# Rotary swap and key duplication by partition copies, one product for a norm's sum, and head norms' squares as float32r pairs

## The chip, the cores and the metric

The kernel runs on one core of a Trainium2 chip. The metric is the time of one execution on the device, in microseconds; the median of several runs counts. Five engines work side by side, each through its own queue in order: TensorE (matrix products; PE in the profile, its weight loads PEld), VectorE (DVE), ScalarE (ACT), GpSimd (POOL) and SyncE (SP), which issues most of the DMAs.

## The reference

Two layers of a diffusion backbone over 256 latent tokens and 256 context tokens, 1024 features. A layer is a half-step SwiGLU, three parallel token mixers with a common input projection, and another half-step SwiGLU. Before each sub-layer stands an RMS norm with a shift and a scale that depend on the condition. In short:

```python
def rmsnorm(x, g):
    return x * lax.rsqrt(jnp.mean(x * x, axis=-1, keepdims=True) + EPS) * g

def adaln(h, m, j, gain):
    return rmsnorm(h, gain) * (1 + m[3 * j + 1]) + m[3 * j]

def apply_rope(x, cos, sin):
    x1, x2 = jnp.split(x, 2, axis=-1)
    return jnp.concatenate([x1 * cos - x2 * sin, x1 * sin + x2 * cos], axis=-1)

# attention: 8 query heads of 64 and 2 key heads, each key head for 4 query heads;
# queries and keys go through rmsnorm over their 64 features, then apply_rope (latent tokens only)
# gated linear attention and mLSTM: 4 heads of 128 each, their outputs go through rmsnorm over 128 features
x = x + 0.5 * m[2] * swiglu(adaln(x, m, 0, g[0]), w13, w2)
x = x + m[5] * mixers(adaln(x, m, 1, g[1]))
x = x + 0.5 * m[8] * swiglu(adaln(x, m, 2, g[2]), w13, w2)
```

In the last layer the context tokens are only needed up to the keys, values and states; its queries, outputs and second half step are computed for the latent tokens alone.

## The kernel before

Features lie on the partitions and the 512 tokens on the columns (`L` = 256 is where the latent tokens begin), so a tile is 128 features by 512 tokens. In the last layer the mixers' outputs and the second half step work on columns 256 to 511 only (`c0 = L`).

Dense products are done as three float32r products (`mm3`, high and low parts of weights and inputs). A weight unit of 128x1024 is loaded by SP, split by ScalarE (`hi`, line 231) and VectorE (`lo`, line 232), and used by 24 products; three units are buffered. Smaller products, and those that form sums over partitions, are plain float32 products through `mm` (lines 149 and 150).

The stages of a layer: the first half step (`ffn`), the mixers (`mixer`), the second half step. In `mixer` the order of the program is: gate columns, gated linear attention (`gla`, two calls that norm two heads each by `head_norm`), the mLSTM (`mlstm`, two calls with two heads each, the same), the first branch of the output projections, values, keys and queries (each tile: a dense product, then `qk_norm`), `attention`, the gates of the attention's branch, the second and third branches, and the output projection. `attention` first makes `kd`, a copy of each key head on both halves of the partitions (product with the table `dup`), and turns `kd` and the four query tiles with `rope`: a product with the permutation table `perm` swaps the halves of 32 features within each head, and VectorE multiplies by the tables of cosine and sine and adds. Scores, softmax and transposes follow for each key head and block of 128 queries.

`square` forms the squares of the residual's eight tiles as they are finished; those of tiles 0 to 5 are added up by GpSimd, and `norm_sums` sums that total and the last two tiles over the features with three products with `ones_d`. `neg2rstd` then takes -2/sqrt of it (Ln, Exp and a Newton step), and `exp_ln_tables` loads ScalarE's table set for it behind the last square. At the end of a phase (`turn`) the last output tiles are computed for the context's columns and then for the latent's, with the next norm behind each, so that one stream's norm lies beside the other's products.

The program text gives data flow and priorities. The framework's scheduler fixes the order of every engine's queue when the program is built, prefers what stands earlier in the text, and fills with later work; it also places the tiles in their pools (the pool `tp` of `W()` has 17 buffers) and sets the semaphores.

Of the kernel before, what the change touches and what calls it, by code (L numbers as in the profile page):

```python
# [9 lines left out]
F32 = mybir.dt.float32  # L10
# [22 lines left out]
# columns of w_in, in the order the kernel consumes them (gate block first)  # L33
# [15 lines left out]
# columns of the small per-layer parameters  # L49
# [8 lines left out]
# shape-only float tables  # L58
CT = {}
# [18 lines left out]
def hybrid_backbone_kernel(ctx: ExitStack, tc: tile.TileContext, xT, cc, small, tables, lmask, crow, modw, modt,  # L78
# [42 lines left out]
    def tt(o, a, b, op):  # L121
        V.tensor_tensor(o, a, b, op)  # L122

    def act(o, i, f, **k):
        return A.activation(o, i, f, **k)  # L125
# [9 lines left out]
    def load(o, i):  # L135
        """a load; those of the start in the order of the program, and some later ones behind them."""
        d = nc.sync.dma_start(o, i)
        if loads and late[0] < 24:
            order(d, loads[-1])
        if starting[0]:  # L140
            loads.append(d)
        else:
            late[0] += 1

    def exp_ln_tables(after):
        """load the table set that serves both Exp and Ln, behind the activation `after`."""
        order(A.preload_act_table_set("natural_log_exp_and_others"), after, "table set of the next functions")  # L147

    def mm(o, l, r, start=True, stop=True):
        PE.matmul(o, l, r, start=start, stop=stop)  # L150

# [1 line left out]
    ct = res.tile([128, N_CT], F32, name="ct")  # L153
# [5 lines left out]
    ones_h = res.tile([128, 128], F32, name="ones_h")  # L159
# [4 lines left out]
    def C(n, i=None, w=128):  # L164
        o, ww = CT[n]
        return ct[:, o:o + ww] if i is None else ct[:, o + i * w:o + (i + 1) * w]
# [19 lines left out]
    V.memset(ones_h[:], 1.0 / 128)  # L186
    V.memset(ones_1[:], 1.0)
    V.memset(onec[:], 0.0)
# [8 lines left out]
    def load_tables():  # L197
        load(ct[:, 130:], tables[:, 130:])
        for i, n in ((0, 4), (4, 3)):
            t = W()  # L200
            load(t[:, :n * 128], lmask[:, i * 128:(i + n) * 128])
            V.tensor_copy(lm[:, i:i + n, :], t[:, :n * 128].rearrange("p (a b) -> p a b", a=n))
        V.tensor_copy(sel[:], C("selm"))

# [1 line left out]
    behind = []  # L206

    class Unit:
        """a run of weight columns as a float32r pair; each part is one tile or a list of tiles of 512."""
# [31 lines left out]
    def wunit_f(src, n, raw=None):  # L241
        """the same in tiles of the feature pool, for units that are wanted ahead of their turn."""
        raw = wraw(src, n) if raw is None else raw
        his, los = [], []
        with tc.high_priority():
            for a in range(0, n, 512):
                m = min(512, n - a)
                hi, lo = F(F32R), F(F32R)
                A.copy(hi[:, :m], raw[:, a:a + m])
                tt(lo[:, :m], raw[:, a:a + m], hi[:, :m].bitcast(F32), ALU.subtract)  # L250
                his.append(hi)
                los.append(lo)
        return Unit(his, los)

    def ahead(srcs):
        """the first two units of the next phase."""
        return [cols8(wunit(srcs[0], 1024)), cols8(wunit_f(srcs[1], 1024))]
# [11 lines left out]
    def dense_with(w, xs, cs):  # L269
        """one tile of 128 output features over the columns cs; K = 128 * len(xs)."""  # L270
        ps = acc()
        for k, x in enumerate(xs):
            mm3(ps[:, cs], w[k][0], w[k][1], x, cs, k == 0, k == len(xs) - 1)
        return ps
# [4 lines left out]
    def dense_halves(ws, xs, done):  # L279
        """some tiles, one stream after the other: starts before the second stream is there."""  # L280
# [9 lines left out]
    def dense_tokens(src, xs):  # L290
        """512 output features with the tokens on partitions: one tile per chunk."""
# [33 lines left out]
    def start(src):  # L325
        """the first norm, the modulation it needs and the first products, as the weights come in."""
# [29 lines left out]
        def features(k):  # L356
            """modulation of the features 128 * k .., then these features of the norm."""
            with tc.high_priority() if k == 0 else ExitStack():
# [9 lines left out]
                for j in range(2):  # L368
                    mm(pt[:, 2 * j:2 * j + 2], sb[:, 128 * j:128 * j + 128], C("sel2"))
# [25 lines left out]
    def load_cond():  # L395
        """silu of the two conditioning vectors, on every partition."""
# [7 lines left out]
    def mod_vec(l, j, cond):  # L404
        """generator: modulation vector j of layer l on the vector engine, 128 features a step."""
# [46 lines left out]
    def mod_scale(l, j):  # L452
        """-0.5 * gain * (1 + scale) of norm j."""
# [7 lines left out]
    def mod_gate(l, j):  # L461
        """half of the gate of sub-layer j."""
# [10 lines left out]
    def neg2rstd(ms, cs, eps_col, eps):  # L473
        """-2 / sqrt(ms + eps): table value with one Newton step."""
# [11 lines left out]
    def square(k, c):  # L486
        """squares of one tile of the stream c, summed over the tiles but the last two."""
# [4 lines left out]
        elif k < KD - 2:  # L492
            G.tensor_tensor(sums[c.start][0][:, c], sums[c.start][0][:, c], q[:, c], ALU.add)
        else:
            sums[c.start].append(q)
# [6 lines left out]
    def adaln(l, j, c0=0):  # L502
        """norm j of layer l: one call of the result for each stream, behind its last residual."""
# [13 lines left out]
    def norm_sums(c, tabled):  # L517
# [4 lines left out]
        for n, q in enumerate(parts):  # L522
            mm(ms[:, c], ones_d[:], q[:, c], n == 0, n == len(parts) - 1)
# [30 lines left out]
    def turn(late, h, gate, nxt):  # L554
        """the last output tiles of a phase by streams, with the norm of the next phase behind each."""
# [11 lines left out]
    def ffn(l, j, c0, fill, pre, xn, side, nxt, head=None):  # L567
        """one half step; pre: the first weights, nxt: where those of the next phase are."""
# [44 lines left out]
    def log_sigmoid(z, bias, out_t, tmp):  # L613
        """log sigmoid(z + bias) = min(z + bias, 0) - ln(1 + exp(-|z + bias|))."""
# [5 lines left out]

    def head_norm(out, o, cs, gcol, eps_col, eps, tabled=True):
        """-2 * rmsnorm over the partitions of o (PSUM), times gcol."""
        sq = W()
        i = act(sq[:, cs], o[:, cs], AF.Square)
        if tabled:
            exp_ln_tables(i)
        ms = mx()
        mm(ms[:, cs], ones_h[:], sq[:, cs])
# [6 lines left out]
    def gla(l, ft, c0, gq, gk, gv, gb, gw2, gcol):  # L635
# [6 lines left out]
        for d in range(2):  # L642
            z = mx()
            mm(z[:], gw2[:, (2 * d + ft) * 128:(2 * d + ft + 1) * 128], gb[:])
# [13 lines left out]
        # states between chunks  # L658
# [3 lines left out]
        for d in range(2):  # L662
# [17 lines left out]
            for i, c in enumerate(ch):  # L680
                ps = mx()
                for hh in range(2):
                    mm(ps[64 * hh:64 * hh + 64, 0:128], kd[:, i * 128 + 64 * hh:i * 128 + 64 * hh + 64],
                       gv[c][:, hd(2 * ft + hh)])
# [7 lines left out]
        # within chunks  # L692
        att = []
        for hh in range(2):
            ps = mx()
            r = slice(64 * hh, 64 * hh + 64)
            for c in range(q0, 4):
                cc_ = slice(c * 128, (c + 1) * 128)
                mm(ps[:, cc_], gk[r, cc_], gq[r, cc_])
# [3 lines left out]
        for li, s in enumerate(LEVELS):  # L703
# [16 lines left out]
            for hh in range(2):  # L720
                ps = mx()
                r = slice(64 * hh, 64 * hh + 64)
                for c in range(q0, 4):
                    cc_ = slice(c * 128, (c + 1) * 128)
                    mm(ps[:, cc_], ek[r, cc_], eq[r, cc_])
# [4 lines left out]
        # outputs  # L730
# [28 lines left out]
    def conv_silu(l, ps, i, c0):  # L759
        """twice silu(conv(x) + b) of one tile of channels."""  # L760
# [18 lines left out]
    def mlstm_rows(l, gb):  # L779
        selgb = C("selgb")  # L780
        pi, pf = mx(), mx()
        mm(pi[:], selgb[:, 0:128], gb[:])
        mm(pf[:], selgb[:, 128:256], gb[:])
# [22 lines left out]
        # columns r = (head parity within direction q, head pair): index 2 * q + hp  # L806
# [9 lines left out]
        # values at the ends of chunks, spread over the partitions  # L816
# [8 lines left out]
        mm(ps[:, 0:64], ones_1[:], dd[:].rearrange("p a b -> p (a b)"))  # L825
# [14 lines left out]
    def mlstm(l, hp, c0, mq, mk, mv, R, gcol):  # L840
# [6 lines left out]
        for hl, h in enumerate(heads):  # L847
            # states between chunks
# [5 lines left out]
            for d in range(2):  # L854
# [7 lines left out]
                for i, c in enumerate(order[d]):  # L862
                    ps = mx()
                    mm(ps[:, 0:129], kt[:, c * 128:(c + 1) * 128], vs[:, i * 129:(i + 1) * 129])
# [7 lines left out]
            # weights within chunks  # L872
            sc = mx()
            for c in range(q0, 4):
                cc_ = slice(c * 128, (c + 1) * 128)
                mm(sc[:, cc_], mk[h][:, cc_], mq[h][:, cc_])
# [10 lines left out]
        # denominators, one row of 32 per (direction, head)  # L887
        den1, qn = mx(), mx()
        for hl in range(2):
            for d in range(2):  # L890
                q = 2 * d + hl
                rr = slice(32 * q, 32 * q + 32)
                mm(den1[rr, cs], onec[:] if hp == 0 else onec2[:], sw[d, hl][:, cs])
                for c in range(q0, 4):
                    cc_ = slice(c * 128, (c + 1) * 128)
                    if c in before[d]:
                        i = before[d][c]
                        # the sum of keys, column 128 of the state, goes to row hp of 32
                        mm(qn[rr, cc_], Cs[d, hl][:, i * 160 + 128 - hp:i * 160 + 160 - hp], mq[heads[hl]][:, cc_])
                    else:  # L900
                        mm(qn[rr, cc_], zero32[:], mq[heads[hl]][:, cc_])
# [36 lines left out]
    def qk_norm(ps, cs, gcol):  # L938
        x, sq = F(), W()
        V.tensor_copy(x[:, cs], ps[:, cs])  # L940
        exp_ln_tables(act(sq[:, cs], x[:, cs], AF.Square))
        ms = mx()
        mm(ms[:, cs], C("blk"), sq[:, cs])
# [4 lines left out]
    def rope(x):  # L948
        ls = slice(L, T)
        ps = mx()  # L950
        mm(ps[:, ls], C("perm"), x[:, ls])
        t = W()
        tt(t[:, ls], ps[:, ls], C("sin"), ALU.mult)
# [3 lines left out]
    def attention(l, c0, aq, kh, vt):  # L957
        ls = slice(L, T)
        kd = []
        for kv in range(2):  # L960
            ps = mx()
            mm(ps[:], C("dup", kv), kh[:])
            t = W()
            A.copy(t[:], ps[:])
# [7 lines left out]
        for kv in range(2):  # L972
            for qt in range(c0 // 128, 4):
# [7 lines left out]
                for j in range(4):  # L981
# [3 lines left out]
                    mm(ps[:, 0:nk], aq[h // 2][r, qc], kd[kv][r, 0:nk])  # L985
# [171 lines left out]
    def beside(l, j, vecs):  # L1157
        """modulation vectors of later sub-layers, computed beside a half step."""
# [25 lines left out]
def _pack(a, mt, kt):  # L1184
    """(K, M) -> [M tile, partition, k * 128 + m]."""
# [3 lines left out]
def _cols(v):  # L1189
    """a vector of n * 128 features as [partition, n]."""  # L1190
# [3 lines left out]
def _tables():  # L1194
# [23 lines left out]
    # queries on partitions, keys on columns  # L1218
# [4 lines left out]
    # source j on partitions, target i on columns  # L1223
# [113 lines left out]
```

## Time and profile before

| | |
|---|---|
| runs, median of 3 | 2334.57 us (2333.76 to 2335.11) |
| profiled execution, first to last instruction (its span) | 2333.1 us |
| median less the profiled span | 1.5 us |
| TensorE with a record of a product | 2291.4 us, 98% |
| VectorE busy | 1533.6 us, 66% |
| ScalarE busy | 975.1 us, 42% |
| GpSimd busy | 53.2 us, 2% |

The profile is of one execution, whose own time is given as its span only. A matrix product's record is longer than its distance to the next one, because products overlap; so the share of TensorE says where it had nothing to do, and what a product costs is read from the distances of the starts. A float32 product shows as two records of the same form.

### The profile page before, as it was taken

The numbers are of one execution on the slowest core, as the hardware profiler recorded it, in microseconds if no ns is written. First come the engines' busy times: TensorE is split into PE (matmuls) and PEld (weight loads), VectorE is DVE, ScalarE is ACT, GpSimd is POOL, SyncE is SP. The second block draws the span as 40 slices with busy tenths as digits, with TensorE's granted clock in tenths as the row PEclk, the third lists the DMA queues.
The fourth block names the chain that finished last, engine by engine and source line by source line (L and its number), as shares of the span: only waits on it lengthen the run. The fifth ranks groups of instructions, "written<-read, shape, count | busy, mean of one in ns | idle before, by whom it ended". The sixth has DMA issues, their size and how long they took to land. (4 is left out here: it accounts for less than half of the span.)

```text
span 2333.1 us, 32827 instructions
## 1 busy us (share of the span) xinstructions
PE 2291.4 (98%) x12496; PEld 1910.3 (82%) x12496; DVE 1533.6 (66%) x3213; ACT 975.1 (42%) x1569; POOL 53.2 (2%) x65
## 2 busy tenths in 40 slices
PE   7999999999999999999999999999999999999999
PEld 4888888777877667888888898888888788889999
DVE  4686875579865664658833357855545897877755
ACT  4322224445644542342222253222245665745443
POOL 0000001000000000100000000000010000001000
PEclk9999999999999999999999999999999999999999
DMA  7665554212211212436533236655433233335764
GB/s 282 210 200 159 187 187 129 91 48 66 82 55 64 64 46 81 147 111 198 173 113 99 76 115 208 202 160 188 157 114 103 88 100 100 109 120 183 241 199 145
DMA packets 117390, 314.94 MB, mean 135 GB/s; under 512 B 13296, under 2 KB 16240, under 8 KB 117104
## 3 DMA queue, kind: packets, MB, share of 16 engines
q1 hardware_dynamic: 116208, 309.69, 41.3%
q0 software_dynamic: 1024, 3.15, 0.4%
q8 instruction: 98, 1.61, 0.3%
q14 instruction: 60, 0.49, 0.1%
HBM read 308.59 MB, written 4.19 MB: 134 GB/s over the span
## 5 line engine op out<-in xcount | busy, mean ns | idle before, releaser
L231 ACT CAST hi<-raw 128x1024 fp32r<-128x1024 f32 (+2 forms) x446 | 434.6, 977 | 962.7 <-PE acc L150 637.4
L150 PE MATMUL acc<-xh,hi 128*128 128x512 f32 (+1 forms) x2192 | 784.5, 358 | 9.6 <-ACT xh L125 6.3
L150 PE MATMUL acc<-xl,hi 128*128 128x512 f32 (+1 forms) x2192 | 783.9, 358 | 0.2
L150 PE MATMUL acc<-xh,lo 128*128 128x512 f32 (+1 forms) x2192 | 781.7, 357 | 1.6 <-DVE lo L232 1.6
L232 DVE TENSOR_TENSOR lo<-raw,hi 128x1024 fp32r<-128x1024 f32 (+2 forms) x446 | 503.4, 1131 | 322.9 <-ACT hi L231 307.7
L150 PEld LDWEIGHTS acc<-xh,hi 128*128 128x128 f32 x2192 | 415.7, 190 | 76.8 <-ACT xh L125 8.7
L150 PEld LDWEIGHTS acc<-xl,hi 128*128 128x128 f32 x2192 | 415.7, 190 | 66.1 <-issue 8.8
L150 PEld LDWEIGHTS acc<-xh,lo 128*128 128x128 f32 x2192 | 415.7, 190 | 64.4 <-issue 6.7
L150 PE MATMUL acc<-f,hi 128*128 128x512 f32 (+1 forms) x1016 | 352.2, 347 | 0.0
L150 PE MATMUL acc<-f,lo 128*128 128x512 f32 (+1 forms) x896 | 314.1, 351 | 0.0
L415 DVE SCALAR_TENSOR_TENSOR u<-f,f 128x512 f32<-128x512 f32 x448 | 284.6, 685 | 12.7 <-DMA f<-in_modt_dram 12.7
L150 PE MATMUL acc<-t,hi 128*128 128x512 f32 (+1 forms) x824 | 287.1, 349 | 0.0
L150 PEld LDWEIGHTS acc<-f,hi 128*128 128x128 f32 x1016 | 192.2, 189 | 25.0 <-issue 1.2
L150 PEld LDWEIGHTS acc<-f,lo 128*128 128x128 f32 x896 | 169.7, 189 | 22.1 <-issue 0.4
L150 PEld LDWEIGHTS acc<-t,hi 128*128 128x128 f32 x824 | 155.8, 189 | 20.3
L122 DVE TENSOR_TENSOR t<-t,acc 128x512 f32<-128x512 f32 (+1 forms) x90 | 54.9, 610 | 154.8 <-PE acc L150 153.7
L539 DVE SCALAR_TENSOR_TENSOR x<-acc,ggt,x 128x256 f32<-128x256 f32 x136 | 61.1, 479 | 88.5 <-PE acc L150 88.4
L125 ACT ACTIVATE t<-t 128x512 f32<-128x512 f32 (+2 forms) x180 | 93.0, 529 | 58.3 <-DVE t L122 35.7
L122 DVE TENSOR_TENSOR t<-t,f 128x512 fp32r<-128x512 f32 (+3 forms) x172 | 99.2, 585 | 2.9 <-ACT f L313 2.1
L150 PE MATMUL mx<-t,t 64*128 64x128 f32 (+2 forms) x592 | 77.9, 288 | 0.9 <-DVE t L861 0.5
L150 PEld LDWEIGHTS mx<-t,t 64*128 64x128 f32 (+1 forms) x592 | 64.2, 188 | 16.3 <-issue 9.1
L150 PE MATMUL mx<-t,f 128*64 128x256 f32 (+3 forms) x352 | 69.8, 412 | 0.4
(209 smaller groups left out, 2167.3 us busy)
## 6 DMA issues: line engine op xcount, KB each, us to landing
raw<-in_w_dram SPq DMA_DIRECT2D x179, 512.0 KB, 3.6
f<-in_modt_dram SPq DMA_DIRECT2D x256, 256.0 KB, 4.5
raw<-in_win_dram SPq DMA_DIRECT2D x118, 512.0 KB, 3.5
raw<-in_w_dram SPq DMA_DIRECT2D x61, 384.0 KB, 3.1
raw<-in_w_dram SPq DMA_DIRECT2D x61, 320.0 KB, 3.0
raw<-in_wout_dram SPq DMA_DIRECT2D x24, 512.0 KB, 3.5
f<-in_modw_dram SPq DMA_DIRECT2D x32, 256.0 KB, 5.3
raw<-in_wo_dram SPq DMA_DIRECT2D x16, 512.0 KB, 3.8
```

What stands on the lines that cost most here:

```text
L122: V.tensor_tensor(o, a, b, op)
L125: return A.activation(o, i, f, **k)
L150: PE.matmul(o, l, r, start=start, stop=stop)
L231: a = A.copy(hi[:, :n], raw[:, :n])
L232: b = V.tensor_tensor(lo[:, :n], raw[:, :n], hi[:, :n].bitcast(F32), ALU.subtract)
L415: V.scalar_tensor_tensor(junk[:], raw[:], 1.0, cond[s][h][:], ALU.mult, ALU.mult, accum_out=part[:, k, s, h:h + 1])
L539: V.scalar_tensor_tensor(X[m][:, c], ps[:, c], gate[:, m, s:s + 1], X[m][:, c], ALU.mult, ALU.add)
```

## The change

`rope` takes the swap of the halves from four GpSimd copies of 32 partitions by 256 columns each, in place of a product. `attention` makes the duplicated keys with two copies of 64 partitions by 512 columns, one on ScalarE and one on GpSimd, in place of a product and a ScalarE copy from PSUM. `square` adds the last two tiles' squares to the total on VectorE, so that `norm_sums` is left with one product. `head_norm` and `qk_norm` write the square twice, once rounded to float32r, subtract to get the low part, and sum over the partitions with two float32r products (`mean_squares`). The tables `perm` and `dup` are no longer loaded (the load is in two parts), `ones_h` and a copy of the table `blk` become float32r. `tt`, `act` and `mm` become names of the engines' functions themselves, and comments go. The start's norm (`start`) is left as it is.

```diff
+    tt, act, mm = V.tensor_tensor, A.activation, PE.matmul
...
-        load(ct[:, 130:], tables[:, 130:])
+        load(ct[:, 130:skip[0]], tables[:, 130:skip[0]])
+        load(ct[:, skip[0]:], tables[:, skip[1]:])
...
+        V.tensor_copy(blk_r[:], C("blk"))
...
     def square(k, c):
         q = W()
         i = act(q[:, c], X[k][:, c], AF.Square)
         if k == 0:
             sums[c.start] = [q]
         elif k < KD - 2:
             G.tensor_tensor(sums[c.start][0][:, c], sums[c.start][0][:, c], q[:, c], ALU.add)
         else:
-            sums[c.start].append(q)
+            tt(sums[c.start][0][:, c], sums[c.start][0][:, c], q[:, c], ALU.add)
...
         ms = mx()
-        for n, q in enumerate(parts):
-            mm(ms[:, c], ones_d[:], q[:, c], n == 0, n == len(parts) - 1)
+        mm(ms[:, c], ones_d[:], parts[0][:, c], True, True)
         return ms
...
+    def mean_squares(x, w, cs):
+
+        sq, hi, lo = W(), W(F32R), W(F32R)
+        act(hi[:, cs], x[:, cs], AF.Square)
+        i = act(sq[:, cs], x[:, cs], AF.Square)
+        tt(lo[:, cs], sq[:, cs], hi[:, cs].bitcast(F32), ALU.subtract)
+        ms = mx()
+        mm(ms[:, cs], w[:], hi[:, cs], True, False)
+        mm(ms[:, cs], w[:], lo[:, cs], False, True)
+        return ms, i
+
     def head_norm(out, o, cs, gcol, eps_col, eps, tabled=True):
-        """-2 * rmsnorm over the partitions of o (PSUM), times gcol."""
-        sq = W()
-        i = act(sq[:, cs], o[:, cs], AF.Square)
+
+        ms, i = mean_squares(o, ones_h, cs)
         if tabled:
             exp_ln_tables(i)
-        ms = mx()
-        mm(ms[:, cs], ones_h[:], sq[:, cs])
...
     def qk_norm(ps, cs, gcol):
-        x, sq = F(), W()
+        x = F()
         V.tensor_copy(x[:, cs], ps[:, cs])
-        exp_ln_tables(act(sq[:, cs], x[:, cs], AF.Square))
-        ms = mx()
-        mm(ms[:, cs], C("blk"), sq[:, cs])
+        ms, i = mean_squares(x, blk_r, cs)
+        exp_ln_tables(i)
...
     def rope(x):
         ls = slice(L, T)
-        ps = mx()
-        mm(ps[:, ls], C("perm"), x[:, ls])
         t = W()
-        tt(t[:, ls], ps[:, ls], C("sin"), ALU.mult)
+        for i in range(4):
+            j = i ^ 1
+            G.tensor_copy(t[32 * i:32 * i + 32, ls], x[32 * j:32 * j + 32, ls])
+        tt(t[:, ls], t[:, ls], C("sin"), ALU.mult)
...
         for kv in range(2):
-            ps = mx()
-            mm(ps[:], C("dup", kv), kh[:])
             t = W()
-            A.copy(t[:], ps[:])
+            for e in range(2):
+                (A.copy if e == kv else G.tensor_copy)(t[64 * e:64 * e + 64, :], kh[64 * kv:64 * kv + 64, :])
             rope(t)
```

## Rows read from the trace of the kernel before

**Rows 1.** Page: span, and engines' busy time, share and instructions.

```profile
span 2333.1 us, 32827 instructions
...
PE 2291.4 (98%) x12496; PEld 1910.3 (82%) x12496; DVE 1533.6 (66%) x3213; ACT 975.1 (42%) x1569; POOL 53.2 (2%) x65
```

**Rows 2.** Windows: stretch, its length, busy us per engine, granted clock, DMA share, GB/s.

```profile
1800.00:1900.00 100.00, 99.45 (x640) 80.22 (x639) 89.12 (x220) 71.28 (x129) 0.00 (x0) 1.00 0.26 83
...
2000.00:2100.00 100.00, 95.92 (x717) 82.53 (x716) 77.03 (x172) 55.31 (x109) 2.16 (x4) 1.00 0.40 122
```

**Rows 3.** Groups by line and shape, TensorE: count, busy us, mean ns, idle before.

```profile
L150 PE MATMUL mx<-t,ones_d 128*128 128x256 f32 x54 | 15.1, 388 | 0.2 <-ACT t L125 0.2
```

**Rows 4.** Timeline, TensorE: start us, length us, names, shape, records merged.

```profile
390.51 0.28 PE L150 MATMUL acc<-f,f 128*128 128x256 f32 x1
390.63 1.02 PE L150 MATMUL mx<-t,ones_d 128*128 128x256 f32 x4
...
391.61 0.28 PE L150 MATMUL acc<-t,hi 128*128 128x256 f32 x1
...
753.78 0.39 PE L150 MATMUL acc<-xh,hi 128*128 128x512 f32 x1
...
754.46 0.39 PE L150 MATMUL acc<-xh,hi 128*128 128x512 f32 x1
754.71 1.13 PE L150 MATMUL mx<-t,ct 128*128 128x512 f32 x2
755.27 0.79 PE L150 MATMUL acc<-xl,hi 128*128 128x512 f32 x1
755.90 0.40 PE L150 MATMUL acc<-xh,lo 128*128 128x512 f32 x1
...
2002.77 0.28 PE L150 MATMUL acc<-xh,lo 128*128 128x256 f32 x1
2002.91 0.70 PE L150 MATMUL mx<-t,ct 128*128 128x256 f32 x2
2003.26 0.47 PE L150 MATMUL acc<-xh,hi 128*128 128x256 f32 x1
2003.57 0.28 PE L150 MATMUL acc<-xl,hi 128*128 128x256 f32 x1
2003.69 0.28 PE L150 MATMUL acc<-xh,lo 128*128 128x256 f32 x1
```

**Rows 5.** Waits, TensorE: who waited for whom, us in total, times, longest.

```profile
PE mx L1006 <- DVE t L999: 6.7, 7, 1.5
...
PE acc L150 <- ACT xh L125: 6.3, 3, 4.1
```

**Rows 6.** Timeline, a turn's first norm, TensorE and ScalarE.

```profile
1369.83 1.28 ACT L147 ACT_TABLE_LOAD   x1
...
1369.87 0.70 PE L150 MATMUL mx<-t,ones_d 128*128 128x256 f32 x2
...
1371.13 0.48 ACT L125 ACTIVATE t<-mx,kc 128x256 f32<-128x256 f32 x1
```

**Rows 7.** Line 493's durations (min/median/max ns); groups by shape, VectorE.

```profile
L493 POOL TENSOR_TENSOR t<-t,t x45: 725/805/1465, 354.0 to 2126.3; 128x256 f32<-128x256 f32 x45
...
L122 DVE TENSOR_TENSOR t<-t 128x256 f32<-128x256 f32 x56 | 20.5, 418 | 0.0
...
L122 DVE TENSOR_TENSOR t<-t,t 128x512 f32<-128x512 f32 x18 | 12.4, 687 | 14.2 <-ACT t L125 14.0
```

**Rows 8.** Layer 1: timeline (key tile's norm, first scores); chain behind the attention.

```profile
1995.57 0.75 DVE L945 SCALAR_TENSOR_TENSOR f<-f,cols,t 128x512 f32<-128x512 f32 x1
...
2018.15 1.13 PE L150 MATMUL mx<-t,f 64*128 64x512 f32 x4
...
2083.93 45.48 PE acc L150 x375
```

More of the change, by code (lines that the diff above doesn't have):

```diff
@@ L119, in mx @@
         return pmx.tile([128, T], F32, tag="mx", name=nm("mx"))
[L121 to L125, printed above, removed]
+    tt, act, mm = V.tensor_tensor, A.activation, PE.matmul
     no_sync = mybir.DependencyInfo(mybir.DependencyClass.NoSync, mybir.DependencyReason.DATA)
@@ L147, in exp_ln_tables @@
         order(A.preload_act_table_set("natural_log_exp_and_others"), after, "table set of the next functions")
-    def mm(o, l, r, start=True, stop=True):
-        PE.matmul(o, l, r, start=start, stop=stop)
-    ct = res.tile([128, N_CT], F32, name="ct")
+    skip = CT["perm"][0], CT["cos"][0]
+    ct = res.tile([128, N_CT - skip[1] + skip[0]], F32, name="ct")
     sel = res.tile([128, 8], F32R, name="sel")
@@ L158, in hybrid_backbone_kernel @@
     ones_d = res.tile([128, 128], F32, name="ones_d")
-    ones_h = res.tile([128, 128], F32, name="ones_h")
+    ones_h = res.tile([128, 128], F32R, name="ones_h")
+    blk_r = res.tile([128, 128], F32R, name="blk_r")
     ones_1 = res.tile([128, 128], F32, name="ones_1")
@@ L165, in C @@
         o, ww = CT[n]
+        o -= skip[1] - skip[0] if o >= skip[1] else 0
         return ct[:, o:o + ww] if i is None else ct[:, o + i * w:o + (i + 1) * w]
@@ L185, in hybrid_backbone_kernel @@
     V.memset(ones_d[:], 1.0 / D)
-    V.memset(ones_h[:], 1.0 / 128)
     V.memset(ones_1[:], 1.0)
+    V.tensor_scalar(ones_h[:], ones_1[:], 1.0 / 128, None, ALU.mult)
     V.memset(onec[:], 0.0)
@@ L368, in features @@
                 for j in range(2):
-                    mm(pt[:, 2 * j:2 * j + 2], sb[:, 128 * j:128 * j + 128], C("sel2"))
+                    mm(pt[:, 2 * j:2 * j + 2], sb[:, 128 * j:128 * j + 128], C("sel2"), True, True)
                 tt(m[:, :, k, :], pt[:, 0:4].rearrange("p (j s) -> p j s", j=2), bias[:, :, k, :].to_broadcast([128, 2, 2]),
@@ L643, in gla @@
             z = mx()
-            mm(z[:], gw2[:, (2 * d + ft) * 128:(2 * d + ft + 1) * 128], gb[:])
+            mm(z[:], gw2[:, (2 * d + ft) * 128:(2 * d + ft + 1) * 128], gb[:], True, True)
             t1, t2, pr = W(), W(), W()
@@ L683, in gla @@
                     mm(ps[64 * hh:64 * hh + 64, 0:128], kd[:, i * 128 + 64 * hh:i * 128 + 64 * hh + 64],
-                       gv[c][:, hd(2 * ft + hh)])
+                       gv[c][:, hd(2 * ft + hh)], True, True)
                 if i == 0:
@@ L698, in gla @@
                 cc_ = slice(c * 128, (c + 1) * 128)
-                mm(ps[:, cc_], gk[r, cc_], gq[r, cc_])
+                mm(ps[:, cc_], gk[r, cc_], gq[r, cc_], True, True)
             a = W()
@@ L724, in gla @@
                     cc_ = slice(c * 128, (c + 1) * 128)
-                    mm(ps[:, cc_], ek[r, cc_], eq[r, cc_])
+                    mm(ps[:, cc_], ek[r, cc_], eq[r, cc_], True, True)
                 V.copy_predicated(chunk_view(att[hh])[:, q0:4, :],
@@ L781, in mlstm_rows @@
         pi, pf = mx(), mx()
-        mm(pi[:], selgb[:, 0:128], gb[:])
-        mm(pf[:], selgb[:, 128:256], gb[:])
+        mm(pi[:], selgb[:, 0:128], gb[:], True, True)
+        mm(pf[:], selgb[:, 128:256], gb[:], True, True)
         ic, tmp, lf, b, m = W(), W(), W(), W(), F()
@@ L824, in mlstm_rows @@
         ps = mx()
-        mm(ps[:, 0:64], ones_1[:], dd[:].rearrange("p a b -> p (a b)"))
+        mm(ps[:, 0:64], ones_1[:], dd[:].rearrange("p a b -> p (a b)"), True, True)
         eb = sp.tile([128, 8, 8], F32, tag="eb", bufs=1, name=nm("eb"))
@@ L863, in mlstm @@
                     ps = mx()
-                    mm(ps[:, 0:129], kt[:, c * 128:(c + 1) * 128], vs[:, i * 129:(i + 1) * 129])
+                    mm(ps[:, 0:129], kt[:, c * 128:(c + 1) * 128], vs[:, i * 129:(i + 1) * 129], True, True)
                     o = i * 160
@@ L875, in mlstm @@
                 cc_ = slice(c * 128, (c + 1) * 128)
-                mm(sc[:, cc_], mk[h][:, cc_], mq[h][:, cc_])
+                mm(sc[:, cc_], mk[h][:, cc_], mq[h][:, cc_], True, True)
             for d in range(2):
@@ L892, in mlstm @@
                 rr = slice(32 * q, 32 * q + 32)
-                mm(den1[rr, cs], onec[:] if hp == 0 else onec2[:], sw[d, hl][:, cs])
+                mm(den1[rr, cs], onec[:] if hp == 0 else onec2[:], sw[d, hl][:, cs], True, True)
                 for c in range(q0, 4):
@@ L897, in mlstm @@
                         i = before[d][c]
-                        mm(qn[rr, cc_], Cs[d, hl][:, i * 160 + 128 - hp:i * 160 + 160 - hp], mq[heads[hl]][:, cc_])
+                        mm(qn[rr, cc_], Cs[d, hl][:, i * 160 + 128 - hp:i * 160 + 160 - hp], mq[heads[hl]][:, cc_], True, True)
                     else:
-                        mm(qn[rr, cc_], zero32[:], mq[heads[hl]][:, cc_])
+                        mm(qn[rr, cc_], zero32[:], mq[heads[hl]][:, cc_], True, True)
         den, nd = W(), W()
@@ L984, in attention @@
                     ps = mx()
-                    mm(ps[:, 0:nk], aq[h // 2][r, qc], kd[kv][r, 0:nk])
+                    mm(ps[:, 0:nk], aq[h // 2][r, qc], kd[kv][r, 0:nk], True, True)
                     if lat:
```

## Prediction

> **What bounds the kernel now.** I read the page's busy table first [rows 1]: TensorE's records cover 2291.4 of the 2333.1 us span, VectorE's 1533.6, and nothing else comes near. Busy time alone doesn't say that TensorE sets the end, since its records overlap, so I looked at the table by stretches [rows 2] and at start-to-start distances [rows 4]. In the two stretches with the attention and its surroundings TensorE is busy 99.45 and 95.92 of 100 us at a granted clock of 1.00 (the 2.4 GHz level), and dense float32r products follow each other every 0.227 us with 512 columns (753.78 to 754.46 is three) and every 0.12 us with 256. That rhythm is the array at work, not a queue at rest. The view of waits [rows 5] names the rest: 41.7 us (2333.1 - 2291.4) without a record, in small pieces; the probabilities before the attention's transposes cost 6.7 us in 7 waits, the modulated input behind a norm 6.3 in 3. So time that is taken out of TensorE's queue comes off the end, unless a new wait eats it; work added to VectorE, ScalarE or GpSimd is free as long as it lies beside the dense stream.
>
> **What a removed product is worth.** A float32 product shows as two records (27 norm products give the 54 records in [rows 3]). Its price in place [rows 4]: alone in a 512-column stream, the product before it is through at 754.46 + 0.227 = 754.69, and the one behind it begins 0.227 before its successor at 755.90, so at 755.67 (the 755.27 that is listed overlaps): 0.98 us. Alone at 256 columns: 2002.77 + 0.12 = 2002.89 to 2003.57 - 0.12 = 2003.45: 0.56 us. Two in a row at 256 columns: 390.51 + 0.12 = 390.63 to 391.61 - 0.12 = 391.49, so 0.43 each, hence 0.86 for 512 (twice the columns). These are the two ends: 0.43 to 0.56, and 0.86 to 0.98. A float32r pair is taken at the dense price: 2 x 0.12 = 0.24, and 2 x 0.227 = 0.45.
>
> **The change, part by part, on TensorE.**
> 1. Norm sums: nine stream norms (two in each of four turns, one in the last mixer) go from three products to one. The two that go stand mostly as a pair: 9 x 0.86 = 7.7 us.
> 2. Rotary swap: 6 calls in each layer, 12 products of 256 columns gone: 12 x 0.43 to 0.56 = 5.2 to 6.7 us.
> 3. Key duplication: 2 in each layer, 4 of 512 columns: 3.4 to 3.9 us.
> 4. Head norms and query/key norms as pairs: 14 of 512 columns (8 heads and 5 query/key tiles in layer 0, the key tile in layer 1) save 0.86 - 0.45 = 0.41 to 0.53 each, 5.7 to 7.4 us; 12 of 256 columns save 0.43 - 0.24 = 0.19 to 0.32, 2.3 to 3.8 us.
>
> The sum is 24.3 to 29.5 us. These products stand singly and in bunches, so I take the middle, 27.
>
> **What it adds elsewhere.** The pairs add a Square on ScalarE and a subtraction on VectorE to each of 26 norms, and the norm sums 18 adds of 0.42 us on VectorE [rows 7]. A subtraction is 0.69 us with 512 columns and 0.42 with 256 [rows 7], so VectorE gets 14 x 0.69 + 12 x 0.42 + 18 x 0.42 = 22 us. Its fullest stretch has 89.12 us of 100 [rows 2]; there it gets the four gate-attention heads of layer 1, under 2 us. Covered by the dense stream; were it not, 2 us come back.
>
> In the chain of a head norm only the first Square is late: the subtraction and both products lie under the table load of 1.28 us that stands behind the second Square. Rows of the same form: the load runs 1369.83 to 1371.11, the Ln starts at 1371.13, and the norm's product, sent at 1369.87, is through some 0.55 later [rows 6]. What is late next, 0.4 to 0.6 us a norm, is a gating or a rotary step that dense tiles cover.
>
> The norm between phases is the delicate one. For a turn's first stream the last square is now followed by an add (0.42 and about 0.1 of hand-over) ahead of the one product: 1369.87 becomes 1370.4, and the product is through at about 1370.95, still before the Ln at 1371.13. For the second stream the pair (0.86) behind the last square becomes add and product (0.42 + 0.1 + 0.43 = 0.95): 0.1 us late. TensorE waits for a norm in three places now, 6.3 us [rows 5]; nine norms at 0.1 are 0.9 us, and if the whole add were bare, 9 x 0.52 = 4.7 us. I take 1.
>
> The table split costs one DMA issue more on SP, early, in the filler beside the first half step; its bytes fall by 384 columns. Nothing waits there, at most one load is a place later. Three work tiles per norm instead of one press on the 17 buffers of that pool; a late buffer delays ScalarE and VectorE, and TensorE only after the dense tiles between. I count nothing, and leave it to a rival.
>
> **The GpSimd copies.** The trace has no such copy. Nearest rows: GpSimd's add of 128x256 takes 0.725 to 1.465 us, median 0.805 [rows 7], with two inputs where a copy has one; from below nothing excludes a tenth of that. I take 0.6 for 32x256 and 1.2 for the 64x512 half of a key tile (twice the columns), and keep 0.1 to 1.47.
>
> GPSIMD Engine Reference of the Trainium skill, section 1, says that GpSimd's SBUF interfaces are shared with VectorE and suffer from its instructions with two SBUF inputs; the spread from 0.725 to 1.465 agrees. Its section 4.1 puts one-input work at about line rate, which at its 1.2 GHz would be an estimate of 0.21 us for 256 columns plus dispatch: the sum would stay as it is.
>
> Is there room? In layer 1 the normed key tile is ready at 1995.57 + 0.75 = 1996.3, and the first scores start at 2018.15 [rows 8], 21.8 us later. Before the first group of four heads GpSimd must do two large copies and the small ones of four rotary calls (both key tiles, two query tiles): 16 small ones and 2 of double length, 20 units. At 0.6 that is 12 us, at 1.47 29 us. Behind the attention TensorE runs 375 products in 45.48 us [rows 8], 0.121 each; the attention's branch (96) and the output projection (192) need it, the other 87, 10.5 us, don't and could be done earlier. So 32.3 us are free, 1.6 us per unit. The swap now also no longer stands in TensorE's queue, where it waited for the query tiles' dense products. I cost the copies at nothing; without the cover each unit's excess over 1.6 us costs 20-fold in layer 1. Layer 0 has more room: tiles twice as wide.
>
> A late copy also blocks VectorE: the multiply by the sine waits for four copies, 2.4 us (5.9 at 1.47), and the weight splits stand behind it. Three weight units are buffered, 24 x 0.12 = 2.9 us each in layer 1, 8.6 us together: covered.
>
> **Sum.** The profiled execution's span is 2333.1, the runs' median 1.5 above it. 2333.1 - 27 + 1 for the norms + 1 for waits that a new order of the queues brings = 2308.1; with 1.5 outside the span 2309.6, say 2309.5.
>
> **Rivals.**
> A, slower: the GpSimd copies are really slow, because moving data to other partitions is another mechanism than its add. It decides in layer 1, between the normed key tile and the first scores: at c us per unit 20c - 32.3 come back. The gain of 25 is gone at c = 2.9. At c = 4 the time is 2309.5 + 48 = 2357. Against it: the longest add is 1.47 [rows 7], half of what it needs; for it: no row shows a copy to other partitions. 6%.
> GPSIMD Engine Reference of the Trainium skill, sections 1 and 3.2, speaks for A: each of GpSimd's eight cores owns 16 partitions in ordinary work, and data goes from one core to another over links of their own. No run here shows such a copy yet.
> B, half the gain: the queues' order is fixed when the program is built, and the longer chains (two Squares, a subtraction, copies, three buffers) make VectorE or ScalarE late by a microsecond or so where TensorE has no cover, as it is before the attention's transposes now [rows 5]. Twelve rotary calls at 1 us bring 12 back: 2321. For it: VectorE is at 77 to 89% there [rows 2]. 16%.
> C, no effect: within 4.7 us of before. It takes the loss of more than four fifths of 27 us, for instance TensorE just waiting at the same places for longer. The rhythm in [rows 4] speaks against it. 4%.
> D, more: an attention that can start earlier also loses some of the 6.7 us before its transposes, and the upper prices hold: 2333.1 - 29.5 - 5 + 1.5 = 2300. 11%.
> My forecast, 2304 to 2316, has the remaining 63%.
>
> **Range and chances.** 2301 to 2324 holds the forecast, most of B and about half of D, 8 in 10. About 0.2% (4.7 us) is what a measurement of this kernel can tell from no change. Faster: forecast, D and B, 90%; same 4%; slower 6%.
>
> **What would show it.** In the changed profile the norm's 256-column records fall from 54 to 18, those of the swap and the duplication are gone, and TensorE's busy time falls by about 25 us with its idle time near 42. GpSimd's busy time rises by 48 small and 4 large copies; around 0.6 us each proves that part, over 1.6 us refutes it. Waits of TensorE for the rotary's last add, for a subtraction behind a Square, or longer ones for the input behind a norm would show B. The prediction is wrong if idle time grows by more than 10 us, or if the pairs cost more than 0.45 and 0.24.

## The result, and the profile after

The change makes the kernel slower: 2348.97 us (median of 4 runs, 2346.93 to 2350.30) against 2334.84 for the kernel before beside it, a ratio of 1.0061 with a 95% interval of 1.0048 to 1.0074. The forecast was 2309.5, and its range ended at 2324.

The page after, span and busy times of the engines, which answers to [rows 1]:

```profile
span 2348.4 us, 32820 instructions
...
PE 2283.8 (97%) x12428; PEld 1905.4 (81%) x12428; DVE 1559.3 (66%) x3258; ACT 990.6 (42%) x1598; POOL 82.9 (4%) x117
```

TensorE's records cover 7.6 us less, and yet the span is 15.3 longer: TensorE is without a record for 64.6 us (2348.4 - 2283.8) instead of 41.7. That is 22.9 more, and a fall in busy time of only 7.6 says that something inside the busy time grew as well. The stretches of the changed kernel say what (length, busy us of each engine, then TensorE's granted clock, DMA share, GB/s):

```profile
2000.00:2100.00 100.00, 88.93 (x647) 76.46 (x646) 76.13 (x159) 62.46 (x116) 16.09 (x28) 0.95 0.37 117
2018.00:2024.00 6.00, 5.07 (x23) 4.96 (x24) 1.60 (x5) 5.79 (x11) 0.00 (x0) 0.50 0.29 90
2024.00:2030.00 6.00, 6.00 (x51) 5.95 (x51) 3.79 (x6) 5.41 (x8) 0.00 (x0) 1.00 0.28 87
```

The stretch that had 95.92 us of TensorE at a clock of 1.00 [rows 2] has 88.93 at 0.95, and inside it lie some microseconds at 0.50 (the 1.2 GHz level), in which 6 us hold 23 products instead of the 51 of the next 6. To add this up I cut the span into windows of 1 us and summed (1 - granted clock) x busy time of TensorE: what its work lost to the lower level. All of it is of one profiled execution of each kernel.

| us | before | after | difference |
|---|---|---|---|
| span | 2333.1 | 2348.4 | +15.3 |
| TensorE without a record | 41.7 | 64.6 | +22.9 |
| lost at half clock while busy | 8.4 | 23.8 | +15.4 |
| rest: work at full clock | 2283.0 | 2260.0 | -23.0 |

So about 23 us of products did go, near the 24.3 to 29.5 that were forecast; 38.3 us of new waits and of half clock ate it. That row of the table is good to some 3 us only: two pairs of the kernels below have the same products on TensorE and differ in it by 2.6 (e3 and e7) and 3.1 (the changed kernel and e4), and in e5, which takes nine float32 products out, it is 0.4 longer than before. The waits of TensorE after (us in total, times, longest), which answer to [rows 5]:

```profile
PE mx L1010 <- DVE t L1003: 13.3, 9, 6.8
PE acc L263 <- ACT xh L527: 10.5, 6, 3.5
...
PE mx L989 <- DVE f L960: 4.1, 1, 4.1
PE acc L263 <- ACT f L1096: 4.0, 2, 3.7
PE acc L1121 <- ACT u L1118: 2.6, 1, 2.6
...
PE acc L263 <- DVE u L1109: 1.9, 1, 1.9
PE mx L520 <- DVE t L493: 1.6, 1, 1.6
```

The first two were 6.7 and 6.3; the others are new, but for the 2.6 at line 1121, which was 1.4. That one is TensorE's wait for ScalarE's copy of the value tile (L1118, at 745 us), which stands behind a head norm in ScalarE's queue. The 1.9 at L1109 comes with the attention's last scores. The rest belong to three places.

**The rotary step.** GpSimd, ScalarE, VectorE and TensorE in layer 1 (start, length, line, names, shape; in brackets the idle time before and what ended it):

```profile
2010.00 0.75 DVE L949 SCALAR_TENSOR_TENSOR f<-f,cols,t 128x512 f32<-128x512 f32 x1
...
2014.99 0.64 POOL L968 COPY t<-f 64x512 f32<-64x512 f32 x1 [283.08 <-PE acc L264]
2015.70 0.92 POOL L957 COPY t<-t 32x256 f32<-32x256 f32 x2
2033.34 0.93 POOL L957 COPY t<-t 32x256 f32<-32x256 f32 x2 [16.73 <-ACT t L968]
2034.33 0.87 POOL L968 COPY t<-f 64x512 f32<-64x512 f32 x1
2035.26 2.89 POOL L957 COPY t<-t 32x256 f32<-32x256 f32 x4
2038.21 8.13 POOL L957 COPY t<-f 32x256 f32<-32x256 f32 x13
...
2032.67 0.61 ACT L968 COPY t<-f 64x512 f32<-64x512 f32 x1
...
2043.78 0.61 DVE L960 TENSOR_TENSOR f<-f,t 128x256 f32<-128x256 f32 x1
...
2044.45 1.23 PE L989 MATMUL mx<-t,f 64*128 64x512 f32 x2 [4.07 <-DVE f L960]
```

The normed key tile is there at 2010.75. GpSimd makes its half of the doubled tile at 2014.99, but ScalarE's half, in ScalarE's queue behind the query norms and the gates, runs at 2032.67. The swap of the doubled tile reads both halves, so GpSimd stands for 16.73 us with all later swaps behind it, and then does the rest in a row. The first scores start at 2044.45 instead of 2018.15 [rows 8]; 14.4 us of that were lost already at the normed key tile (2010.75 for 1996.3), and not all of the rest is the late half, as e2 and e4 below show. Layer 0 has the same picture with 16.06 us. The copies themselves are cheap:

```profile
L957 POOL COPY t<-f 32x256 f32<-32x256 f32 x32 | 17.5, 548 | 1.5
...
L968 POOL COPY t<-f 64x512 f32<-64x512 f32 x4 | 3.3, 821 | 666.2 <-DVE t L479 383.0 <-PE acc L264 283.1
```

**The second stream's norm.** From its last residual to its Ln, in the kernel before:

```profile
1378.75 0.47 DVE L539 SCALAR_TENSOR_TENSOR x<-acc,ggt,x 128x256 f32<-128x256 f32 x1
...
1380.75 0.47 ACT L125 ACTIVATE t<-mx,kc 128x256 f32<-128x256 f32 x1 [0.19 <-PE mx L150]
```

and in the changed one:

```profile
1380.15 0.48 DVE L536 SCALAR_TENSOR_TENSOR x<-acc,ggt,x 128x256 f32<-128x256 f32 x1
1380.55 0.87 DVE L528 SCALAR_TENSOR_TENSOR xl<-t,mod,xh 128x256 fp32r<-128x256 f32 x2
1381.34 0.87 DVE L526 SCALAR_TENSOR_TENSOR t<-x,gsc,t 128x256 f32<-128x256 f32 x2
1382.13 0.95 DVE L493 TENSOR_TENSOR t<-t,t 128x256 f32<-128x256 f32 x2
...
1380.69 0.71 ACT L487 ACTIVATE t<-x 128x256 f32<-128x256 f32 x2
...
1383.13 0.70 PE L520 MATMUL mx<-t,ones_d 128*128 128x256 f32 x2
...
1383.87 0.47 ACT L474 ACTIVATE t<-mx,kc 128x256 f32<-128x256 f32 x1 [1.10 <-PE mx L520]
```

2.0 us become 3.7. The squares are over at 1381.40, but both adds stand in VectorE's queue behind the first stream's modulation (L526, L528) until 1382.13; products of TensorE needed no place in that queue.

**The gates.** ScalarE and TensorE in the changed kernel, layer 1:

```profile
2013.13 0.40 ACT L621 ACTIVATE t<-f 128x256 fp32r<-128x256 f32 x1
2013.44 0.40 ACT L622 ACTIVATE t<-f 128x256 f32<-128x256 f32 x1
2013.86 1.28 ACT L143 ACT_TABLE_LOAD   x1
...
2017.20 1.28 ACT L1096 ACT_TABLE_LOAD   x1
2018.50 0.38 ACT L1096 ACTIVATE f<-acc 128x256 f32<-128x256 f32 x1
...
2018.93 0.58 PE L263 MATMUL acc<-xh,hi 128*128 128x256 f32 x1 [3.66 <-ACT f L1096]
...
2020.14 0.41 PE L263 MATMUL acc<-xh,hi 128*128 128x256 f32 x1
2020.35 0.41 PE L264 MATMUL acc<-xl,hi 128*128 128x256 f32 x1
```

The gates' Tanh, which frees the accumulator that TensorE wants, comes late in ScalarE's queue, behind a query norm with its two Squares. Behind this wait, in the stretch at 0.50 above, the products follow each other every 0.21 us instead of 0.12 [rows 4].

### The profile page after: what moved, and what is told of

Same layout as the page of the kernel before. It is cut to its first block, busy times and chain, and to the rows that moved or that the text cites. A ratio compares the mean times of both kernels' runs of the same rounds, so it can differ in the third digit from the quotient of the medians.

```text
span 2348.4 us, 32820 instructions
## 1 busy us (share of the span) xinstructions
PE 2283.8 (97%) x12428; PEld 1905.4 (81%) x12428; DVE 1559.3 (66%) x3258; ACT 990.6 (42%) x1598; POOL 82.9 (4%) x117
## 5 line engine op out<-in xcount | busy, mean ns | idle before, releaser
L263 PE MATMUL acc<-xh,hi 128*128 128x512 f32 (+1 forms) x2192 | 785.3, 358 | 18.1 <-ACT xh L527 10.5
L263 PE MATMUL acc<-f,hi 128*128 128x512 f32 (+1 forms) x896 | 312.6, 350 | 2.8 <-DVE u L1109 1.9
L264 PE MATMUL acc<-t,hi 128*128 128x512 f32 (+1 forms) x704 | 248.7, 353 | 0.0
L263 PEld LDWEIGHTS acc<-f,hi 128*128 128x128 f32 x896 | 169.3, 189 | 26.6 <-DVE u L1109 2.1
L264 PEld LDWEIGHTS acc<-t,hi 128*128 128x128 f32 x704 | 133.1, 189 | 18.1
L491 POOL TENSOR_TENSOR t<-t,t 128x256 f32<-128x256 f32 x45 | 44.1, 998 | 1125.4 <-ACT t L487 1125.4
L264 PE MATMUL acc<-x,hi 128*128 128x512 f32 (+1 forms) x192 | 64.7, 339 | 0.0
L311 ACT CAST f<-t 128x512 fp32r<-128x512 f32 (+1 forms) x92 | 51.5, 560 | 13.6 <-DVE t L548 11.9
L527 ACT ACTIVATE xh<-t,mod 128x256 fp32r<-128x256 f32 x88 | 40.4, 503 | 38.8 <-DVE t L526 38.7
L312 DVE TENSOR_TENSOR t<-t,f 128x512 fp32r<-128x512 f32 (+1 forms) x90 | 54.7, 607 | 1.6 <-ACT f L311 1.6
```

The costliest lines, as they stand in the source:

```text
L263: mm(o, wh, xh[:, cs], start=first, stop=False)
L264: mm(o, wh, xl[:, cs], start=False, stop=False)
L311: A.copy(hi[:, cs], src[:, cs])
L312: tt(lo[:, cs], src[:, cs], hi[:, cs].bitcast(F32), ALU.subtract)
L527: a = act(xh[:, c], t[:, c], AF.Identity, bias=sh[:, k, s:s + 1])
```

## The experiments

Ratios are to the kernel before in the same session, with their 95% intervals; a loss or gain in us is the ratio applied to 2335 us, unless medians are named.

**One part alone, three times.** The norm sums alone (e1), both kinds of pairs alone (e2), the copies alone (e3):

```
-            sums[c.start].append(q)
+            tt(sums[c.start][0][:, c], sums[c.start][0][:, c], q[:, c], ALU.add)
...
+        mm(ms[:, c], ones_d[:], parts[0][:, c], True, True)
```

> The kernel before with the norm's sum in one product alone. Theory N (the two adds on VectorE stand behind the other stream's modulation, so each second stream's norm comes 1 to 1.7 us later and TensorE waits for it four or five times): 7.7 us of products go, 5 to 7 come back, 2333 (2331 to 2336). The prediction's own step (0.1 us late per norm): 2328.

> The kernel before with the float32r pairs of the head norms and the query/key norms alone (the blk table only as its float32r copy, to make room). Theory P (the second Square and the subtraction make the mixers' chain late by some 10 us in layer 1, until the dense fill is used up and TensorE waits behind the attention): 2334 to 2342, first scores of layer 1 at least 8 us later within the mixer. Theory C (the copies alone are at fault): the pairs save 8 to 11 us, 2325.

> The kernel before with the swap and the key duplication by copies alone. Theory C (GpSimd's queue stands behind the half that ScalarE copies late, and 24 copies in a row then delay the first scores): 2336 to 2345, with a wait of GpSimd of over 10 us for ScalarE's copy. Theory P: the copies are covered, 8.6 to 10.6 us of products go, 2325.

Measured: e1 2336.30, 1.0011 (1.0001 to 1.0020); e2 2343.73, 1.0047 (1.0030 to 1.0063); e3 2339.58, 1.0031 (1.0018 to 1.0044). None of the three parts gains anything. e3 lies inside theory C's range, e1 0.3 us above theory N's and e2 1.7 above theory P's, and the step of the prediction that e1 put to the test (2328) is out. Each loses at a place of its own: e1 has the 10.5 us of waits for xh that the changed kernel has, e2 a wait of 3.66 us for the gates, and e3 the wait for ScalarE's half of the key tile (TensorE's waits and GpSimd's row of e3):

```profile
PE mx L1009 <- DVE t L1002: 13.5, 7, 7.0
...
PE mx L150 <- DVE f L122: 5.7, 1, 5.7
...
2015.84 1.53 POOL L956 COPY t<-t 32x256 f32<-32x256 f32 x2 [13.74 <-ACT t L967]
```

2.5 us of the profiled execution of e2 are half clock at 35 to 40 us, where the pairs are not yet in use; its other executions were as slow (2341.81 to 2345.12). Its first scores of layer 1 start at 2038.85, 20.7 us later than before, without any copy.

**The key halves.** Is it ScalarE's half, or GpSimd? The changed kernel with both halves on GpSimd (e4), and the kernel before with swap and duplication as copies, all on GpSimd (e7):

```
-                (A.copy if e == kv else G.tensor_copy)(t[64 * e:64 * e + 64, :], ...)
+                G.tensor_copy(t[64 * e:64 * e + 64, :], ...)
```

> The changed kernel with both halves of the duplicated keys copied by GpSimd, so that its queue waits for no ScalarE copy. Theory C: most of the loss in the attention goes, 2332 to 2337. Theory P (the query norms themselves are late): at most 5 us better than the changed kernel, 2344 to 2349.

> The kernel before with the swap and the duplication by copies, all of them on GpSimd. Theory C (the copies were only costly through the half on ScalarE, for which GpSimd's queue stood): 8.6 to 10.6 us of products go and the waits of 7.0 and 5.7 us before the attention vanish, 2322 to 2327. Rival (the 24 copies in a row are too long for the front of the attention): 2332 or more, the wait for the rotary's last add stays.

Measured: e4 2335.65, 1.0007 (0.9998 to 1.0017); e7 2324.66, 0.9964 (0.9951 to 0.9977). Theory C holds in both. One engine's name in one line is worth 12.6 us in the changed kernel (1.0061 - 1.0007), and 15.6 between e3 and e7. GpSimd in e7 starts right behind the normed key tile (1988.39) and does layer 1's copies almost in one go:

```profile
1988.55 2.16 POOL L967 COPY t<-f 64x512 f32<-64x512 f32 x2 [266.55 <-DVE f L948]
...
1994.98 2.79 POOL L956 COPY t<-t 32x256 f32<-32x256 f32 x4
1997.83 8.70 POOL L956 COPY t<-f 32x256 f32<-32x256 f32 x12
```

e7 is faster than both kernels: by 8.4 us against the kernel before. Its profiled execution was its fastest: of the 11.8 us that its span is shorter, 7.5 are work (forecast for the 16 products: 8.6 to 10.6), 0.7 idle time and 3.6 half clock.

Where the 12.6 us lie can be read between waits that all kernels have, in profiled executions that are 18.6 us apart (e4's is among its fastest). From the one for the value tile near 745 to the one for xh near 1020, in layer 0, the kernel before takes 273.1 us, the changed one 276.8 and e4 267.4. From the one near 1781 to the last mixer's for xh near 2140, in layer 1, it is 354.5, 368.3 and 360.6. So the late half cost 9.4 us in layer 0, more than that stretch lost, and 7.7 in layer 1, where e4 still loses 6.1. There the pairs of the query norms make the first scores late as well: they start 21.8 us behind the normed key tile before, 33.7 in the changed kernel, 30.7 in e4, and 32.1 in e2, which has the pairs and no copy.

**The norm with two products.** If VectorE's queue is what makes e1's add late, GpSimd, which adds the other squares anyway, could take tile 6, and the last square keep its product; alone (e5), and on e7 (e8):

```
-        elif k < KD - 2:
+        elif k < KD - 1:
             G.tensor_tensor(sums[c.start][0][:, c], sums[c.start][0][:, c], q[:, c], ALU.add)
```

> The kernel before with tile 6's square added by GpSimd too, so that a norm's sum has two products: the total and the last square, with no add behind the last square. Theory N (the add behind VectorE's modulation was the cost): 3.9 us of products go and no wait grows, 2328 to 2331. Rival (fewer products don't shorten the turns at all): 2333 or more.

> All copies on GpSimd and the norm's sum in two products, no float32r pairs. If theories C and N hold and the two add up: 2318 to 2323, faster than both kernels. If either fails: 2328 or more.

In both the theory fails and the other branch comes: e5 2337.27, 1.0015 (1.0006 to 1.0025); e8 2331.51, 0.9986 (0.9977 to 0.9996), which is 6.9 behind e7 by the medians. The stretch with the norm, from the first 128x256 product to the first 128x512 one behind it, is a measure that half clock elsewhere doesn't touch (us, three turns, the first product near 382, 999 and 1360):

| | products per stream's norm | lengths |
|---|---|---|
| before | 3 | 30.6, 28.7, 30.5 |
| e7 | 3 | 30.6, 28.7, 30.5 |
| e1 | 1, adds on VectorE | 31.0, 29.7, 31.4 |
| e5 | 2, add on GpSimd | 31.6, 30.0, 32.0 |

The stretch grows although products leave it: its end is set by the second stream's chain, not by TensorE's work. In e5 that chain has GpSimd's add in it (a wait of TensorE in e5):

```profile
PE mx L150 <- POOL t L493: 1.5, 3, 0.5
```

**The norm of the first stream alone** (e9): its add has the table load to hide it.

```
         elif k < KD - 2:
             G.tensor_tensor(...)
+        elif c.start == 0:
+            tt(sums[c.start][0][:, c], sums[c.start][0][:, c], q[:, c], ALU.add)
```

> The kernel before with the rotary swap and the key halves as GpSimd copies, and the norm sum in one product for the first stream alone; the second stream keeps its three products. Theory (the product of a norm can go where another wait hides the two VectorE adds: the first stream's Ln waits for a 1.28 us table load anyhow, the second stream's stands at the end of the stretch with nothing in front of it): 2319 us, 2316 to 2322, ratio 0.993 to 0.9955, and the stretch from 128x256 to 128x512 products around 1360 us is 0.4 to 0.9 us shorter than 30.5. Rival (TensorE waits at the end of the stretch for the second stream's modulated tiles, so that any product taken out ahead of them comes back as a wait): 2324 to 2327, ratio 0.996 to 0.9975, the stretch 30.3 to 30.8 with a longer wait for xh at its end.

Measured: 2325.73, 0.9967 (0.9955 to 0.9980), the same as e7 within the intervals; the rival held. The stretches are 30.1, 28.5 and 30.6: the first stream's products go, and TensorE waits for the second stream instead (1.67 us at 1015.76, where e7 waits 1.19).

**The pairs.** Only the head norms (e6), and then the same extra work without its use (e10): each head norm also computes the rounded square and the rest, behind the square, and the float32 product stays.

```
+        sq, hi, lo = W(), W(F32R), W(F32R)
         i = act(sq[:, cs], o[:, cs], AF.Square)
+        act(hi[:, cs], o[:, cs], AF.Square)
+        tt(lo[:, cs], sq[:, cs], hi[:, cs].bitcast(F32), ALU.subtract)
```

> The kernel before with the pairs in the 16 head norms alone, the query and key norms as before. Theory P (the added Square and subtraction make the mixers' chain late): the head norms of layer 1 come 5 us or more later and the time is 2334 to 2340. Theory Q (only the query and key norms' pairs cost): the head norms' products save 4 to 6 us, 2327 to 2330.

> The kernel before, in which each head norm also computes the rounded square on ScalarE and the rest on VectorE, behind the square that its float32 product still reads; nobody reads the two. The chain to the product is as before, the two engines have all the work of the pairs. Theory O (the pairs cost by the time that they take in ScalarE's and VectorE's queues, in which other work stands behind them): slower than the head pairs alone by the 6 to 8 us of products that stay, 2341 to 2347, ratio 1.003 to 1.0055, with a wait of 2 to 4 us for the gates at about 2010 to 2020. Theory L (they cost by the two links that they put between the accumulator and the product): 2333 to 2337, ratio 0.9995 to 1.001, and no wait over 1.5 us at the gates.

Measured: e6 2338.77, 1.0015 (1.0006 to 1.0025); e10 2339.32, 1.0022 (1.0012 to 1.0032). e6 lies in theory P's range; e10 lies between its two theories, and its wait for the gates is 1.5, where O set 2 to 4 and L none above 1.5. Waits of TensorE in e6, then in e10 (ACT f: the gates; ACT u: the copy of the value tile):

```profile
PE acc L150 <- ACT f L125: 3.9, 1, 3.9
PE acc L1124 <- ACT u L1121: 2.6, 1, 2.6
```

```profile
PE acc L1119 <- ACT u L1116: 3.3, 1, 3.3
...
PE acc L150 <- ACT f L125: 1.5, 1, 1.5
```

The distance between two places that both have tells the layers apart, again in one profiled execution of each. In layer 0, from the wait near 444 to the one near 1021, the kernel before takes 576.3 us, e6 577.2, e10 580.3. In layer 1, from the wait near 1781 to the last mixer's near 2135, it takes 354.5, e6 361.0, e10 355.6. Half clock by the 1 us windows is 1.5, 4.5 and 4.5 us of these in layer 0, of which e6 and e10 lost 1.3 each more than the kernel before behind the very first wait, which is as long in all three and stands ahead of this layer's pairs. Without that, layer 0 costs 2.7 with the extra work alone and -0.4 with the pairs: the cheaper products there pay for the work and little more. In layer 1 the first wait is again as long in all three, and e6 lost 1.3 more behind it, e10 0.2 less. Without that, the work alone costs 1.3, and putting it between the accumulator and the product 3.9 more. By these executions the queues' time weighs more in layer 0 and the two links in layer 1; neither theory holds for both.

## Why the prediction was wrong

The miss is 39.5 us (2348.97 - 2309.5), and the experiments part it. The late half of the key tile is 12.6 of it (e4). The norm's sum and the pairs, which were to save 15.7 to 18.9, cost 10.0 on top of copies that are all on GpSimd (e4 against e7, 1.0007 - 0.9964); that is the rest, some 27.

**TensorE's saving: about right in sum, one term over-sized.** 24.3 to 29.5 forecast, 23.0 found, to some 3 us. By the same account e1 lost 5.8 us of work (7.7 forecast), e7 7.5 and e3 10.1 (8.6 to 10.6), e2 only 4.2 where 8.0 to 11.2 stood: in e2's trace the next product starts 0.23 to 0.44 us behind a pair's 512-column product and not always 0.227, so a pair costs more than the 0.45 that the sum took.

**"I cost the copies at nothing": the step that failed first.** Their price was no higher than the estimate (0.6 and 1.2 estimated, 0.55 and 0.82 measured on average), and rival A, slow copies, is refuted. What the sum left out is in the diff: one half of each key tile is ScalarE's. The 20 units were laid end to end behind the normed tile as if GpSimd had only itself to wait for; the sum asked how long GpSimd works and never when its input is there. ScalarE copied late before as well, 14.7 us behind the normed tile (1996.3), from a product that itself came 11.4 behind it:

```profile
2007.72 1.02 PE L150 MATMUL mx<-f,ct 128*128 128x512 f32 x2
...
2010.99 0.57 ACT L964 COPY t<-mx 128x512 f32<-128x512 f32 x1
```

but then only the keys stood behind it. The swaps were products in TensorE's queue, and the change put all of them behind that copy. That is worth 12.6 us (e4): without it the changed kernel is within 1.6 us of the kernel before.

GPSIMD Engine Reference of the Trainium skill, sections 1 and 3.2, spoke for rival A (each core owns 16 partitions, links between the cores move data across partitions). The runs speak against it: these copies took 0.55 us on average (median 0.49), below GpSimd's own add with its median of 0.805 [rows 7].

**"0.1 us late" for the norm's second stream: wrong by 1.6.** The add was costed with a hand-over of 0.1, as if VectorE were free. It has the first stream's modulation in its queue there, and the chain went from 2.0 to 3.7 us. The 4.2 us more of waits for xh are near the 4.7 that I named for a bare add and didn't take. The removed products had next to no worth in the first place: e9 shows that the stretch nearly keeps its length when TensorE has less to do in it.

**The pairs "lie under the table load" and the rest is "covered by the dense stream": wrong.** The load covers one norm's chain, but ScalarE runs the norms one after the other, and the gates' Tanh behind them frees an accumulator. e2 shows 11.0 us of loss for the pairs alone, e6 a loss of 3.5 for those of the head norms, and e10 that the same work off the chain, in the two queues only, goes with a loss too (5.1, in part chance, as said below).

**Half clock: missing from the sum.** 15.4 us, as much as the whole loss. Every wait was priced at its own length, and the windows of the changed kernel show a stretch at 0.50 behind most new waits of 1.3 us and more: 2.8 us lost behind the 2.62 at 745, 2.5 behind the 6.76 at 807, 2.5 behind the 3.66 at 2019, 3.0 behind 1.94 and 1.29 at 2103 to 2105. Not behind all: none is lost behind the 1.30 at 1752.

Rival B named this mechanism (longer chains make ScalarE and VectorE late where TensorE has no cover) and gave it 16% and 12 us; its waits came to 22.9, and the 15.4 of half clock stand in no rival. The signs set down for it came: the wait for the rotary's last add (4.07), the longer ones for the input behind a norm (10.5 for 6.3), and idle time up by more than 10. The parts alone lose 2.6, 11.0 and 7.2 us, 20.8 together, and the change 14.2. That the parts share waits at the same places would fit, but it was not taken apart.

What stays open: how much of e10's 5.1 us its unused work causes. Its profiled execution has no more idle time than the kernel before (41.7); its 5.2 us are half clock (13.7 us for 8.4), of which 2.1 lie before 40 us and 1.3 behind the wait near 444, both ahead of any head norm. That is not all chance: the executions of e10 with a mean granted clock of 0.996 or 0.997 took 2335.55 to 2337.86 us, those of the kernel before in that session 2331.57 to 2333.04.

## What to carry to other kernels

Taking work from the engine that is the bound gains only where its end, and not a chain beside it, sets the stretch: measure the stretch, as in the norm here, before pricing the product. When a step moves from one in-order queue to another, ask for each of its inputs when it is ready and what stands behind the first one that is late; here a half-tile copy on the wrong engine cost 12.6 us. Price a new TensorE wait of more than a microsecond above its length if the trace shows half clock behind the waits that are there: here 15.4 us came on top of 22.9, though not every such wait was followed by it.

## What the runs showed that I had not expected

The same wait can cost nothing or 3 us more. Between 443 and 447 us TensorE waits 3.12 or 3.13 us in every kernel; in the next microseconds the granted clock differs from one profiled execution to the next. The kernel before, e1 and e7:

```profile
445.00:450.00 5.00, 5.00 (x20) 4.04 (x20) 3.07 (x9) 1.41 (x3) 0.00 (x0) 0.79 0.05 20
```

```profile
445.00:450.00 5.00, 5.00 (x16) 4.03 (x15) 2.78 (x11) 1.81 (x3) 0.00 (x0) 0.50 0.12 47
```

```profile
445.00:450.00 5.00, 4.94 (x23) 3.98 (x23) 1.75 (x4) 1.25 (x2) 0.00 (x0) 1.00 0.29 87
```

By the 1 us windows, from the wait on, this lost 1.5, 2.9 and 0 us. The executions of one and the same kernel spread along with it: of 26 runs of the kernel before, the shortest (2331.20 us) had a mean granted clock of 0.997, the longest (2338.89) 0.993.

GpSimd's copies to other partitions are cheaper than its add (medians 0.49 and 0.805 us), and four times the elements (64x512 against 32x256) took 1.5 times as long: 821 and 548 ns.
